# A two-layer float32 model on one Trainium2 core: the second layer's projections by seven block products, and one pass over chunks for queries, gates, u and retention

## The chip, the cores and the metric

The program runs on one core of one Trainium2 chip. The metric is device time of one execution in microseconds (us). Besides its runs, each kernel has one profiled execution, whose trace is read here. Engines: PE is TensorE, DVE VectorE, ACT ScalarE, POOL GpSimd; SP only issues DMAs.

## What is computed

Two layers over 2048 tokens of width 1024, all in float32. The first (pooling, two attentions, a gated feed-forward of width 2816) is touched only at its end. The second is this, cut down; its input is the output of the first layer, normalized once more:

```python
h = rmsnorm_2(x, g_pre) * (1.0 + scale[:, None, :]) + shift[:, None, :]
proj = jnp.einsum('bsd,de->bse', h, w_in)            # 1024 -> 7 x 512
gu, gv, gg, rq, rk, rv, rg = jnp.split(proj, PROJ_SPLITS, axis=-1)
# gmlp_branch, per chunk of 128 tokens and 4 groups of 128 channels
v = group_layernorm(v, ln_g); ws = w_s * causal[None]
mixed = jnp.einsum('gts,bnsgd->bntgd', ws, v) + b_s.T[None, None, :, :, None]
y_gmlp = u * mixed * jax.nn.silu(gate)
# retention_branch, 4 heads of 128
q = rotary(q, positions); k = rotary(k, positions) * (Dh ** -0.5)
scores = jnp.einsum('bnqhd,bnkhd->bhnqk', q, k) * decay_mask
intra = jnp.einsum('bnhqk,bnkhe->bnqhe', scores, v)
kv_chunk = jnp.einsum('bnkhd,bnkhe,kh->bnhde', k, v, k_decay)
def step(state, kv): return state * chunk_decay + kv, state
cross = jnp.einsum('bnqhd,bnhde,qh->bnqhe', q, states, q_decay)
y_ret = group_layernorm(intra + cross, gn_g) * jax.nn.silu(gate)
y = jnp.concatenate([y_gmlp, y_ret], axis=-1)
y = rmsnorm_2(jnp.einsum('bsm,md->bsd', y, w_out), g_post)
return x + gate[:, None, :] * y
```

## The kernel before

Every large product is made of three: both operands are split into a high and a low part (`split`, L123: ACT copies the high part, DVE subtracts it for the low one), and high x high, high x low and low x high are added up in PSUM. A product of 128 tokens, 1024 inputs and 512 columns is thus 24 matmuls of 128x512 (`mm3`, L148, lines L153 to L155, through `dense_N`).

The feed-forward (`phase2`) makes its products with `seven` (L995): a two by two block product by seven block products instead of eight. Its left side are seven stationary parts `l` (`stationary`, L970: three differences and one sum, seven splits, for each step of 256 tokens), its right side seven moving parts `r` (`moving`, L928: differences of the weight or activation blocks, L936, and fourteen splits of two k-blocks of 512), which stay for a whole group. The line of its matmuls is L1005; a step with 1024 inputs and two results of 512 columns for two token tiles is 84 matmuls. The partial sums are added by DVE (L1023, L1025, and in the `use` functions), and in `down` also by POOL (L1181). Each `r` part has one buffer, so at a change of the moving parts (a swap) the new part can be written only after the last product with the old one. `hidden` runs two halves of the tokens, `down` three groups of input channels (`FGROUPS`) by eight steps. Side work is put after products through the list `self.later`.

The second layer (`phase3`) goes by four blocks of 512 tokens (`second`, after `second_in` and `second_T`, which normalize, transpose (L194) and split). In each block the seven projections follow one another (`project`: gate, v, u, k, v, q, retention gate); their weights are loaded and split for every block (`wgroup`, tiles `ws`). Between them stand the mix (L1401) and, per chunk, the retention: heads transposed (L1430), scores (L1451), masked by DVE (L1454), cross product with the state (L1460), intra product (L1462), state update (L1470, L1474), group norm (L1323, L1324, POOL's root L175, L1486). The result is transposed (L1395) and the output projection is plain too (L1514 squares, L1515 gain, L1526 final sum). In this layer PE's work is 3456 matmuls of 128x512.

Who comes first on an engine is settled when the program is built, by a scheduler with priorities; each engine then runs its list in order.

## Time and profile before

| | before |
|---|---|
| three runs, median (lowest, highest) | 3651.73 us (3647.63, 3655.74) |
| profiled execution | 3649.51 us |
| its span in the trace | 3647.7 us |
| mean granted PE clock | 0.975 |
| PE busy | 94% |
| DVE, ACT, POOL busy | 67%, 43%, 25% |
| DMA traffic, mean | 516.77 MB, 142 GB/s |

Shares of busy time are means over stages. A matmul is recorded longer than the distance to the next one, since they overlap; to count what PE could do, the distance between starts is taken. The granted clock is given as a part of full speed; 0.5 is the lower of two levels, 1.2 GHz for 2.4.

### The profile page before, as it was taken

The numbers are of one execution on the slowest core, as the hardware profiler recorded it, in microseconds if no ns is written. First come the engines' busy times: TensorE is split into PE (matmuls) and PEld (weight loads), VectorE is DVE, ScalarE is ACT, GpSimd is POOL, SyncE is SP. The second block draws the span as 40 slices with busy tenths as digits, with TensorE's granted clock in tenths as the row PEclk, the third lists the DMA queues.
The fourth block names the chain that finished last, engine by engine and source line by source line (L and its number), as shares of the span: only waits on it lengthen the run. The fifth ranks groups of instructions, "written<-read, shape, count | busy, mean of one in ns | idle before, by whom it ended". The sixth has DMA issues, their size and how long they took to land. (4 is left out here: it accounts for less than half of the span.)

```text
span 3647.7 us, 46845 instructions
## 1 busy us (share of the span) xinstructions
PE 3435.5 (94%) x16704; PEld 2837.7 (78%) x16704; DVE 2455.8 (67%) x4104; ACT 1551.5 (43%) x2874; POOL 911.8 (25%) x1153
## 2 busy tenths in 40 slices
PE   6989989998889989999999998999969999999998
PEld 5777868887667877888778887878758878888887
DVE  8566674768888837666796668686856554655444
ACT  5346574657667634333433334232333332333322
POOL 4322243325652111110200002343521120221101
PEclk9999999999989999999999999999989999999999
DMA  5367655555433444333272334555563252332421
GB/s 168 122 208 225 184 158 179 191 156 179 149 107 113 136 145 143 104 101 110 94 233 75 104 118 136 171 177 172 182 230 115 70 180 87 129 125 75 159 90 64
DMA packets 397915, 516.77 MB, mean 142 GB/s; under 512 B 32449, under 2 KB 250225, under 8 KB 397681
## 3 DMA queue, kind: packets, MB, share of 16 engines
q1 hardware_dynamic: 357152, 384.73, 34.5%
q0 software_dynamic: 40528, 129.04, 9.9%
q8 instruction: 132, 2.16, 0.2%
q14 instruction: 103, 0.84, 0.1%
HBM read 385.98 MB, written 127.69 MB: 141 GB/s over the span
## 5 line engine op out<-in xcount | busy, mean ns | idle before, releaser
L1005 PE MATMUL acc<-r,l 128*128 128x512 f32 x6384 | 1477.9, 393 | 49.3 <-ACT l L126 8.8
L1005 PEld LDWEIGHTS acc<-r,l 128*128 128x128 f32 x6384 | 1203.9, 189 | 313.7 <-ACT l L126 14.8
L153 PE MATMUL d<-ws,h 128*128 128x512 f32 (+1 forms) x1280 | 508.5, 400 | 4.5 <-ACT b L1383 3.5
L154 PE MATMUL d<-ws,h 128*128 128x512 f32 (+1 forms) x1280 | 498.5, 391 | 0.0
L155 PE MATMUL d<-ws,h 128*128 128x512 f32 (+1 forms) x1280 | 496.4, 390 | 0.0
L127 DVE TENSOR_TENSOR ws<-raw,ws 128x1024 fp32r<-128x1024 f32 x216 | 272.9, 1266 | 217.4 <-ACT ws L126 214.2
L126 ACT ACTIVATE l<-sf 128x512 fp32r<-128x512 f32 (+1 forms) x312 | 192.9, 621 | 494.8 <-PE acc L1005 320.3
L126 ACT ACTIVATE ws<-raw 128x1024 fp32r<-128x1024 f32 x216 | 229.1, 1061 | 300.7 <-PE d L155 160.0
L126 ACT ACTIVATE l<-raw 128x512 fp32r<-128x512 f32 (+1 forms) x234 | 144.0, 618 | 361.2 <-PE acc L1005 353.3
L666 PE MATMUL s<-k,q 128*128 128x512 f32 (+2 forms) x960 | 272.7, 394 | 21.6 <-DVE s L697 6.2
L127 DVE TENSOR_TENSOR l<-sf,l 128x512 fp32r<-128x512 f32 (+1 forms) x312 | 234.3, 754 | 75.6 <-ACT l L126 73.6
L153 PEld LDWEIGHTS d<-ws,h 128*128 128x128 f32 x1280 | 243.2, 190 | 50.6 <-ACT b L1383 4.3
L155 PEld LDWEIGHTS d<-ws,h 128*128 128x128 f32 x1280 | 242.6, 190 | 48.6
L154 PEld LDWEIGHTS d<-ws,h 128*128 128x128 f32 x1280 | 243.2, 190 | 44.8 <-issue 1.0
L127 DVE TENSOR_TENSOR l<-raw,l 128x512 fp32r<-128x512 f32 (+1 forms) x234 | 174.8, 752 | 95.4 <-ACT l L126 95.2
L666 PEld LDWEIGHTS s<-k,q 128*128 128x128 f32 x960 | 167.2, 198 | 59.5 <-DVE s L697 14.1
L793 DVE TENSOR_TENSOR_SCAN s<-s,one 128x512 f32<-128x512 f32 (+3 forms) x160 | 188.2, 1208 | 21.6 <-ACT s L789 15.2
L1107 POOL DMA_DIRECT2D act<-wk x88 | 48.4, 550 | 583.8 <-DVE wk L1106 576.4
L704 ACT ACTIVATE s<-s,mx 128x128 f32<-128x128 f32 (+15 forms) x128 | 154.4, 1207 | 81.4 <-DVE mx L700 80.4
L725 PE MATMUL o<-v,pT 128*128 128x128 f32 x1088 | 149.3, 278 | 8.4 <-ACT pT L733 6.1
L725 PEld LDWEIGHTS o<-v,pT 128*128 128x128 f32 x1088 | 140.7, 193 | 19.4 <-ACT pT L733 10.3
L801 POOL TENSOR_TENSOR s<-s,s 128x1024 f32<-128x1024 f32 x48 | 123.5, 2573 | 72.7 <-DVE s L793 45.8
(277 smaller groups left out, 5330.8 us busy)
## 6 DMA issues: line engine op xcount, KB each, us to landing
raw<-in_w_in_dram SPq DMA_DIRECT2D x172, 512.0 KB, 4.2
raw<-in_w_out_dram SPq DMA_DIRECT2D x64, 512.0 KB, 4.3
k<-qkd SPq DMA_DIRECT2D x120, 256.0 KB, 4.2
q<-qkd SPq DMA_DIRECT2D x96, 256.0 KB, 4.4
wk<-x SPq DMA_DIRECT2D x96, 256.0 KB, 5.1
x<-wk POOLq DMA_DIRECT2D x96, 256.0 KB, 3.1
raw<-in_w_gate_dram SPq DMA_DIRECT2D x44, 512.0 KB, 3.8
...
```

Of the source, the lines that this page charges most:

```text
L126: nc.scalar.activation(hi, src, AF.Copy)
L127: nc.vector.tensor_tensor(out=lo, in0=src, in1=hi.bitcast(F32), op=ALU.subtract)
L153: self.nc.tensor.matmul(ps, st(0), mv(0), start=i == 0, stop=False)
L154: self.nc.tensor.matmul(ps, st(0), mv(1), start=False, stop=False)
L155: self.nc.tensor.matmul(ps, st(1), mv(0), start=False, stop=i == n - 1)
L666: nc.tensor.matmul(ps[:, :w], q[:, hl, c * P:(c + 1) * P], kt[:, o:o + w], start=hl == 0, stop=hl == 1 and not extra)
L704: nc.scalar.activation(e[:, :nk], e[:, :nk], AF.Exp, scale=-1.0, bias=mx[:, m, np_ - 1:np_], accum_out=s1[:, c, m:m + 1])
L725: nc.tensor.matmul(ops[:, c * P:(c + 1) * P], pT[:, j * P:(j + 1) * P], vs[kt // NT][:, kt % NT], start=kt == 0, stop=kt == nt - 1)
L793: nc.vector.tensor_tensor_scan(out=omb[:, c, :w][:, ::-1], data0=omb[:, c, :w][:, ::-1], data1=self.one.to_broadcast([P, w]), initial=1.0 ...
L801: nc.gpsimd.tensor_tensor(out=beta[:, two], in0=beta[:, two], in1=omb[:, two, 1:w + 1], op=ALU.mult)
L1005: nc.tensor.matmul(ps, l[lk][:, a, k], r[rk][:, b, k], start=first and k == 0 and i == 0, stop=k == nk - 1 and i == 2, skip_group_check=no ...
L1107: nc.gpsimd.dma_start(out=dst[:, j * TB:(j + 1) * TB], in_=s)
```

## The change

The second layer is cut anew. (1) Normalizing, transposing and writing its input (`h3_d`) is done by `second_rows`, as side work in the last group of `down` and in the first two steps after it. (2) `keys_values` makes the key and value projections with `seven` in eight steps of 256 tokens, rotates the keys and stores both. (3) `spatial` makes the gate and v projections of the gMLP with `seven`, and the mix, and stores the product with the gate. (4) The new `phase3` holds the split weights of q, retention gate and u in SBUF and makes one pass over sixteen chunks of 128 tokens: three plain products of 24 matmuls, and the retention of the chunk. (5) `phase4` makes the output projection with `seven`, with the final norm and sum. Besides, `moving` takes its blocks in another order and makes all differences on DVE, a piece of side work may spread over several products, and `FGROUPS` is turned round, so that the last group of `down` has eight blocks of 128 inputs.

```diff
-FGROUPS = (8, 8, 6)
+FGROUPS = (6, 8, 8)
...
             self.phase2()
-            self.pri.update(w=1000, x=1000)
             self.phase3()
+            self.phase4()
...
+        a = get(0, 0)
+        r["11"] = part("11", a)
+        b = get(0, 1)
+        less(a, b, a)
+        r["t1"] = part("t1", a)
+        for p in range(len(pieces)):
+            (c, n), u = pieces[p], get(1, 1, p)[0]
+            for o in (a[p], b[p]):
+                nc.vector.tensor_tensor(out=o[:, :n], in0=u[:, :n], in1=o[:, :n], op=ALU.subtract)
+        r["t2"] = part("t2", a)
+        r["t3"] = part("t3", b)
         r21 = get(1, 0)
-        if not first:
-            r["21"] = part("21", r21)
-            r["22"] = part("22", r22)
-        t4 = t2
-        less(t4, r21, t2, nc.gpsimd)
-        r["t4"] = part("t4", t4)
+        r["21"] = part("21", r21)
+        less(a, r21, a)
+        r["22"] = part("22", get(1, 1))
+        r["t4"] = part("t4", a)
...
-            for f in todo:
-                f()
+            self.later = [g for g in todo if next(g, None)] + self.later
...
+            self.load_rows()
             for g in range(len(FGROUPS)):
                 self.down(g)
+            self.keys_values()
+            self.spatial()
...
+            else:
+                self.l = self.second_stationary(self.h3_d, 0)
...
-        if not last_g:
-            with self.tc.high_priority(500):
-                self.r = self.down_moving(g + 1)
+            if last_g and s < n - 2:
+                self.later.append(self.second_rows(s))
+        with self.tc.high_priority(500):
+            self.r = self.down_moving(g + 1) if not last_g else self.second_moving("w_in_2", 4 * TB, 5 * TB)
...
+    def token_steps(self, src, use, follow, rows=False):
+        nc = self.nc
+        for s in range(S // (2 * P)):
+            l, r = self.l, self.r
+            if s < S // (2 * P) - 1:
+                self.l = self.second_stationary(src, s + 1)
+            elif follow is not None:
+                self.l = follow[0]()
+            if rows and s < 2:
+                self.later.append(self.second_rows(6 + s))
+            def total(i, j, keep=False):
+                def f(z, ps):
+                    o = self.t(self.wk, [P, TB], "wk") if keep else z
+                    nc.vector.tensor_tensor(out=o, in0=ps, in1=z, op=ALU.add)
+                    use(2 * s + i, j, o)
+                return f
+            self.seven(l, r, KC // 2, lambda ps: use(2 * s, 0, ps), total(0, 1), total(1, 0), total(1, 1, True))
+        self.flush()
+        if follow is not None:
+            with self.tc.high_priority(500):
+                self.r = follow[1]()
+    def keys_values(self):
+        nc = self.nc
+        wk = lambda: self.t(self.wk, [P, TB], "wk")
+        def use(t, j, o):
+            psum = t % 2 == 0 and j == 0
+            if j == 0:
+                d = wk()
+                self.rotate(d, t, o, wk(), not psum)
+                o = d
+            nc.gpsimd.dma_start(out=(self.kr_d, self.vr_d)[j][t], in_=o)
+        self.token_steps(self.h3_d, use, (lambda: self.second_stationary(self.h3_d, 0), lambda: self.second_moving("w_in_2", 2 * TB, TB)), True)
+    def spatial(self):
...
+            if j == 1:
+                mv = self.group_stats([o[:, g * P:(g + 1) * P] for g in range(4)], "gs")
+                r = self.rsqrt_mean(mv[:, :, 1], 4, 1.0)
...
+                nc.gpsimd.tensor_tensor(out=off, in0=mv[:, :, 0], in1=r[:, :4], op=ALU.mult)
...
+                for g in range(4):
+                    c = o[:, g * P:(g + 1) * P]
+                    nc.scalar.activation(c, c, AF.Identity, scale=r[:, g:g + 1], bias=off[:, g:g + 1])
+                nc.gpsimd.tensor_tensor(out=o, in0=o, in1=lng, op=ALU.mult)
+            else:
...
+                nc.scalar.activation(s, o, AF.Silu)
...
+            have[t, j] = o
+            if (t, 1 - j) in have:
+                v, g_ = have.pop((t, 1)), have.pop((t, 0))
+                def mix():
+                    ps = self.t(self.tp2, [P, TB], "tp2")
+                    for g in range(4):
+                        c = slice(g * P, (g + 1) * P)
+                        nc.tensor.matmul(ps[:, c], wsT[:, c], v[:, c], start=True, stop=True)
+                    for g in range(4):
+                        c = slice(g * P, (g + 1) * P)
+                        nc.vector.scalar_tensor_tensor(out=g_[:, c], in0=ps[:, c], scalar=bs[:, g:g + 1], in1=g_[:, c],
+                                                       op0=ALU.add, op1=ALU.mult)
+                    nc.gpsimd.dma_start(out=self.m_d[t], in_=g_)
+                self.later.append(once(mix, 4))
+        self.token_steps(self.h3_d, use, None)
...
+    def phase3(self):
...
+            def queries(t):
+                x = self.token_tile(self.h3_d, t, self.rawh, "rawh")
+                h = self.t(self.hl3, [P, 2, KC, P], "hl", F32R, align=512)
+                self.split(h[:, 0], h[:, 1], x)
+                kr, vv, m, q = (tmp() for _ in range(4))
+                for o, src in ((kr, self.kr_d), (vv, self.vr_d), (m, self.m_d)):
+                    nc.sync.dma_start(out=o, in_=src[t])
+                self.rotate(q, t, product("q", h), tmp(), False)
+                return h, kr, vv, m, q
+            new, last = queries(0), None
+            for t in range(n):
+                h, kr, vv, m, q = new
+                gate = tmp()
+                def gates():
+                    nc.scalar.activation(gate, product("g", h), AF.Silu)
+                    nc.gpsimd.tensor_tensor(out=gate, in0=gate, in1=self.gng, op=ALU.mult)
+                def units():
+                    nc.vector.tensor_tensor(out=m, in0=product("u", h), in1=m, op=ALU.mult)
+                if t < n - 1:
+                    gates()
+                steps = self.retention(q, kr, vv, t == n - 1)
+                next(steps)
+                if last is not None:
+                    self.chunk_out(*last)
+                if t < n - 1:
+                    units()
+                next(steps)
+                if t < n - 1:
+                    new = queries(t + 1)
+                else:
+                    units()
+                    gates()
+                self.turned(t, 0, m)
+                y = drain(steps)
+                last = t, y, gate
+            self.chunk_out(*last)
...
+        kT, qT = heads_T(kr), heads_T(q)
+        for h, c in enumerate(H if not end else ()):
+            nc.gpsimd.tensor_scalar(out=kr[:, c], in0=kr[:, c], scalar1=self.kdec[:, h:h + 1], scalar2=None, op0=ALU.mult)
+        sp = self.t(self.pm, [P, TB], "m")
+        for c in H:
+            nc.tensor.matmul(sp[:, c], kT[:, c], qT[:, c], start=True, stop=True)
+        sT = tmp()
+        nc.vector.tensor_tensor(out=sT, in0=sp, in1=self.ret_mask.rearrange("p h q -> p (h q)"), op=ALU.mult)
+        yield
+        op = self.t(self.pm, [P, TB], "m")
+        old = self.state
+        if old is not None:
+            for h, c in enumerate(H):
+                nc.tensor.matmul(op[:, c], qT[:, c], old[:, c], start=h == 0, stop=False)
+        new = None
+        if not end:
             kp = self.t(self.pm, [P, TB], "m")
+            new = self.t(self.tmp, [P, TB], "state", bufs=2)
+        for h, c in enumerate(H if not end else ()):
+            nc.tensor.matmul(kp[:, c], kr[:, c], vv[:, c], start=True, stop=True)
+            if old is None:
+                nc.vector.tensor_copy(new[:, c], kp[:, c])
+            else:
+                nc.vector.scalar_tensor_tensor(out=new[:, c], in0=old[:, c], scalar=CHUNK_DECAY[h], in1=kp[:, c], op0=ALU.mult,
+                                               op1=ALU.add)
+        self.state = new
+        for h, c in enumerate(H):
+            nc.tensor.matmul(op[:, c], sT[:, c], vv[:, c], start=old is None and h == 0, stop=h == RH - 1)
+        yield
+        y = tmp()
+        nc.scalar.activation(y, op, AF.Copy)
+        mv = self.group_stats([y[:, c] for c in H], "rn")
+        vq = self.t(self.tiny, [P, 4], "vq")
+        nc.gpsimd.tensor_tensor(out=vq, in0=mv[:, :, 1], in1=self.qdec2, op=ALU.mult)
...
+    def phase4(self):
+        nc, a = self.nc, self.a
+        with ExitStack() as es:
+            self.block_pools(es, last=True)
+            with self.tc.high_priority(700):
+                self.l = self.second_stationary(self.yT_d, 0)
+            with self.tc.high_priority(500):
+                self.r = self.second_moving("w_out_2", 0, TB)
+            gout = self.t(self.c3, [P, D], "wide")
...
                 junk = self.t(self.tiny, [P, TB], "junk3", mybir.dt.bfloat16, bufs=1)
+                nc.scalar.activation(junk, src, AF.Square, scale=D ** -0.5, accum_out=ss[:, j:j + 1])
+                nc.vector.tensor_tensor(out=y[:, c], in0=src, in1=gout[:, c], op=ALU.mult)
...
+                nc.gpsimd.tensor_scalar(out=m, in0=ss[:, 0:1], scalar1=ss[:, 1:2], scalar2=EPS, op0=ALU.add, op1=ALU.add)
+                nc.gpsimd.tensor_tensor(out=r, in0=m, in1=self.mhalf[:, :1], op=ALU.pow)
+                for h in range(2):
+                    c = slice(h * TB, (h + 1) * TB)
+                    nc.vector.scalar_tensor_tensor(out=y[:, c], in0=y[:, c], scalar=r, in1=res[:, c], op0=ALU.mult, op1=ALU.add)
+                    (nc.sync if t >= S // P - 2 else nc.gpsimd).dma_start(out=self.out[0, t * P:(t + 1) * P, c], in_=y[:, c])
...
+            self.token_steps(self.yT_d, use, None)
```

Line numbers of the new program are its own: `split` is L133 and L134, `less` and the differences L949 and L980, `stationary`'s sums L1001, `seven` L1025, L1042 and L1044, the plain products L160 to L162.

**PE where the second layer starts.** `acc` are PSUM tiles, `pp` those of the transposes, `d` those of the plain products. Before, after the last products of `down`:

```order
L1005 MATMUL acc_23646<-r_22747,l_23542 128x512 x9
L1005 MATMUL acc_23710<-r_22752,l_23547 128x512 x9
L1005 MATMUL acc_23682<-r_22759,l_23550 128x512 x9
L194 MATMUL pp_23871<-c_ident,x_23825 128x128
L194 MATMUL pp_23871<-c_ident,x_23827 128x128
L194 MATMUL pp_23871<-c_ident,x_23829 128x128
L194 MATMUL pp_23871<-c_ident,x_23831 128x128
L153 MATMUL d_23973<-ws_23955,h_23876 128x512
```

Now, where `down` gives way to keys and values (the `r` tiles are the new moving parts, `l_241` are stationary parts of the first step, `l_243` of the second):

```order
L1025 MATMUL acc_24516<-r_24358,l_24135 128x512
L1025 MATMUL acc_24632<-r_24309,l_24372 128x512 x12
L1025 MATMUL acc_24401<-r_24347,l_24130 128x512 x5
L1025 MATMUL acc_24653<-r_24320,l_24377 128x512 x12
L1025 MATMUL acc_24516<-r_24358,l_24135 128x512 x11
L1025 MATMUL acc_24666<-r_24333,l_24382 128x512 x12
L1025 MATMUL acc_24471<-r_24363,l_24138 128x512 x12
L1025 MATMUL acc_24702<-r_24338,l_24387 128x512 x12
L1025 MATMUL acc_24747<-r_24358,l_24395 128x512 x12
```

Transposes of the layer's input, which stood between `down` and the first projection, are gone from the seam, and products of the second step stand between those of the first.

**DVE inside the retention.** `d` is a plain product, `m` a small one, `ws` and `hl` are splits. Before, around one chunk:

```order
L1474 SCALAR_TENSOR_TENSOR state_28395<-state_26896,m_28394 128x128
L1421 TENSOR_TENSOR tmp_28452<-tmp_28452,tmp_28453 128x4x64
L1422 TENSOR_TENSOR tmp_28452<-tmp_28452,tmp_28453 128x4x64
L127 TENSOR_TENSOR ws_28707<-raw_28705,ws_28707 128x1024
L1464 TENSOR_SCALAR b_28011<-b_28011,c_ret_kdec 128x128 x4
L127 TENSOR_TENSOR ws_28939<-raw_28937,ws_28939 128x1024
L1323 BN_STATS rn_s_28405<-b_28013 128x6 x4
L1474 SCALAR_TENSOR_TENSOR state_28395<-state_26896,m_28394 128x128
L1454 TENSOR_TENSOR tmp_28477<-m_28472,c_ret_mask 128x512
L1419 TENSOR_TENSOR tmp_28550<-d_28525,c_cos 128x512
L1420 TENSOR_TENSOR tmp_28551<-d_28525,c_sin 128x512
L1324 BN_AGGR rn_m_28406<-rn_s_28405 128x2 x4
```

Now, one chunk of the pass:

```order
L1597 SCALAR_TENSOR_TENSOR state_29297<-state_29113,m_29296 128x128
L1405 TENSOR_TENSOR tmp_29318<-d_29322,rot_6184_29348 128x512
L1406 TENSOR_TENSOR tmp_29347<-d_29322,rot_6185_29350 128x512
L1407 TENSOR_TENSOR tmp_29318<-tmp_29318,tmp_29347 128x4x64
L1408 TENSOR_TENSOR tmp_29318<-tmp_29318,tmp_29347 128x4x64
L1472 BN_STATS rn_s_29366<-tmp_29364 128x6 x4
L1597 SCALAR_TENSOR_TENSOR state_29297<-state_29113,m_29296 128x128
L1473 BN_AGGR rn_m_29367<-rn_s_29366 128x2 x4
L1611 TENSOR_SCALAR tmp_29364<-tmp_29364,rn_m_29367,vq_29376 128x128 x4
L1558 TENSOR_TENSOR tmp_29364<-tmp_29364,tmp_29203 128x512
L1597 SCALAR_TENSOR_TENSOR state_29297<-state_29113,m_29296 128x128
L1581 TENSOR_TENSOR tmp_29438<-m_29433,c_ret_mask 128x512
```

The splits of weights are gone; rotation, statistics, norm (L1611), product with the gate (L1558), last state update (L1597), mask (L1581) and the product with u (L1526) of one chunk stand in one row.

**DVE ahead of the output projection.** `r` and `stg` are moving parts and their blocks, `raw_63` the first stationary blocks. Before, from the last retention norm to the first output tile:

```order
L1474 SCALAR_TENSOR_TENSOR state_30374<-state_30307,m_30373 128x128
L1496 TENSOR_TENSOR b_29729<-b_29729,rg_30535 128x512
L127 TENSOR_TENSOR ws_30590<-raw_30588,ws_30590 128x1024
L1474 SCALAR_TENSOR_TENSOR state_30374<-state_30307,m_30373 128x128
L127 TENSOR_TENSOR ws_30707<-raw_30705,ws_30707 128x1024
L127 TENSOR_TENSOR y_30543<-tp_30538,y_30543 128x512
L127 TENSOR_TENSOR y_30551<-tp_30546,y_30551 128x512
L127 TENSOR_TENSOR y_30559<-tp_30554,y_30559 128x512
L127 TENSOR_TENSOR y_30567<-tp_30562,y_30567 128x512
L1515 TENSOR_TENSOR b_30570<-d_30593,c_gout 128x512
```

Now, from the last chunk's statistics to the first split of a stationary part:

```order
L1472 BN_STATS rn_s_30410<-tmp_30408 128x6 x4
L134 TENSOR_TENSOR r_30593<-stg_30535,r_30593 128x1024
L1473 BN_AGGR rn_m_30411<-rn_s_30410 128x2
L949 TENSOR_TENSOR stg_30537<-stg_30575,stg_30537 128x1024
L1473 BN_AGGR rn_m_30411<-rn_s_30410 128x2 x3
L134 TENSOR_TENSOR r_30577<-stg_30575,r_30577 128x1024
L134 TENSOR_TENSOR r_30588<-stg_30584,r_30588 128x1024
L134 TENSOR_TENSOR r_30593<-stg_30537,r_30593 128x1024
L1611 TENSOR_SCALAR tmp_30408<-tmp_30408,rn_m_30411,vq_30420 128x128 x4
L134 TENSOR_TENSOR r_30588<-stg_30586,r_30588 128x1024
L1558 TENSOR_TENSOR tmp_30408<-tmp_30408,tmp_30307 128x512
L1001 TENSOR_TENSOR sf_30509<-raw_6377_30504 128x512
```

Where four splits of finished outputs and a few of weights stood, there are now five splits and a difference of moving parts, the end of the last chunk, and the stationary parts of the first step.

## Rows read from the trace of the kernel before

**Rows 1.** Page, the span and busy time by engine (us, share of the span, instructions).
```profile
span 3647.7 us, 46845 instructions
...
PE 3435.5 (94%) x16704; PEld 2837.7 (78%) x16704; DVE 2455.8 (67%) x4104; ACT 1551.5 (43%) x2874; POOL 911.8 (25%) x1153
```

**Rows 2.** Stretches: from:to, us, busy us of each engine (instructions), PEclk, DMA share, GB/s.
```profile
2584.00:2680.00 96.00, 96.00 (x424) 79.06 (x423) 72.06 (x114) 26.23 (x51) 42.52 (x49) 1.00 0.61 199
2680.00:2734.00 54.00, 24.32 (x98) 17.41 (x97) 28.85 (x33) 20.51 (x33) 10.75 (x15) 0.68 0.70 254
2734.00:2964.00 230.00, 226.14 (x1088) 186.63 (x1088) 131.23 (x256) 79.28 (x116) 37.24 (x52) 1.00 0.37 119
```

**Rows 3.** Groups of PE, 2686 to 3648: count, busy us, mean ns, idle before.
```profile
L153 PE MATMUL d<-ws,h 128*128 128x512 f32 x896 | 354.8, 399 | 3.8 <-ACT b L1383 3.5 <-ACT h L126 0.3
...
L153 PE MATMUL d<-ws,y 128*128 128x512 f32 x256 | 101.2, 395 | 4.5 <-DVE b L1515 3.8 <-ACT y L126 0.3
...
L1460 PE MATMUL m<-state,tmp 128*128 128x128 f32 x120 | 22.0, 279 | 1.1 <-DVE state L1474 1.1
...
L1401 PE MATMUL m<-b,c_wsT 128*128 128x512 f32 x32 | 15.0, 592 | 0.0
```

**Rows 4.** Timeline of PE: start us, us, engine, line, operation, count [idle before <-releaser].
```profile
2685.11 1.78 PE L1005 MATMUL acc<-r,l 128*128 128x512 f32 x4
2707.83 0.48 PE L194 MATMUL pp<-c_ident,x 128*128 128x128 f32 x1 [20.94 <-DVE x L1341]
...
2805.15 1.03 PE L1395 MATMUL tp<-c_ident,b 128*128 128x128 f32 x8
...
3108.27 1.06 PE L1462 MATMUL m<-b,tmp 128*128 128x128 f32 x8
...
3640.74 0.39 PE L155 MATMUL d<-ws,y 128*128 128x512 f32 x1
```

**Rows 5.** Stretches around the four changes of the moving parts, columns as in group 2.
```profile
1790.00:1850.00 60.00, 52.98 (x229) 42.12 (x228) 60.00 (x68) 26.64 (x39) 18.98 (x7) 1.00 0.51 168
2240.00:2285.00 45.00, 35.55 (x145) 27.57 (x144) 40.85 (x47) 15.23 (x23) 20.91 (x15) 0.96 0.68 218
2395.00:2435.00 40.00, 34.14 (x133) 26.67 (x132) 38.88 (x39) 17.80 (x24) 19.74 (x12) 0.91 0.53 171
2555.00:2600.00 45.00, 41.01 (x175) 31.98 (x174) 43.04 (x57) 17.82 (x31) 23.75 (x20) 1.00 0.45 147
```

**Rows 6.** Groups of DVE and POOL: three in `down` (2430 to 2555), three in a block (2734 to 2964).
```profile
L127 DVE TENSOR_TENSOR l<-sf,l 128x512 fp32r<-128x512 f32 x27 | 22.8, 849 | 10.6 <-ACT l L126 10.5
L127 DVE TENSOR_TENSOR l<-raw,l 128x512 fp32r<-128x512 f32 x20 | 18.3, 937 | 0.1
...
L1181 POOL TENSOR_TENSOR wk<-wk,wk 128x512 f32<-128x512 f32 x21 | 29.7, 1424 | 38.5 <-DMA wk<-x 20.0 <-DVE wk L1025 18.3
...
L175 POOL TENSOR_TENSOR rs_r<-rs_m,mhalf 128x4 f32<-128x4 f32 x10 | 10.7, 1070 | 0.8
...
L1323 DVE BATCH_NORM_STATS2 gs_s<-b 128x6 f32<-128x128 f32 x16 | 3.5, 278 | 0.7 <-ACT b L1372 0.6
...
L1324 DVE BATCH_NORM_AGGREGATE gs_m<-gs_s 128x2 f32<-128x6 f32 x16 | 1.6, 155 | 0.0
```

**Rows 7.** Timelines: PE at the swap inside `down`, POOL and DVE at the swap inside `hidden`.
```profile
2407.66 9.42 PE L1005 MATMUL acc<-r,l 128*128 128x512 f32 x33 [2.92 <-DVE wk L1175]
...
1809.70 6.77 POOL L936 TENSOR_TENSOR stg<-stg,stg 128x1024 f32<-128x1024 f32 x1 [10.44 <-DVE r L127]
...
1808.41 3.48 DVE L127 TENSOR_TENSOR r<-stg,r 128x1024 fp32r<-128x1024 f32 x3
1811.81 0.68 DVE L127 TENSOR_TENSOR l<-sf,l 128x512 fp32r<-128x512 f32 x1
1812.41 0.68 DVE L127 TENSOR_TENSOR l<-raw,l 128x512 fp32r<-128x512 f32 x1
...
1814.75 2.80 DVE L127 TENSOR_TENSOR r<-stg,r 128x1024 fp32r<-128x1024 f32 x1
```

423 lines of the change are left out of this document (185 added, 238 removed).

## The prediction

> **What bounds the kernel now.** The page comes first: TensorE (PE) is busy 94% of a span of 3647.7 us [rows 1], so the time is first a count of matmuls and then what PE loses between them. The table by stretches shows where [rows 2]: in the last group of `down`, and in a whole block of the second layer, PE is full (96.00 of 96, 226.14 of 230), while VectorE (DVE) has 72.06 of 96 and 131.23 of 230. Only the seam between the two, 2680 to 2734, has PE at 24.32 of 54 and a granted clock of 0.68. So DVE, ScalarE (ACT) and DMA are off the path inside the stages and on it at seams.
>
> **The price of a matmul.** In the full stretch of `down` 424 starts of 128x512 stand in 96 us [rows 2], 0.2264 each; I take 0.227, which allows for a record that is missing. Eight records of the small F32 kind take 1.06 us of which the last one's 0.28 laps over, so 0.112 a record, two records to a product; eight transposes take 1.03 with 0.27, so 0.109 each [rows 4].
>
> **The second layer now.** The last products of `down` end at 2685.11 + 1.78 = 2686.9 [rows 4], the last of them having started some 0.6 before; from that start, 2686.3, to the end of the span at 3647.7 are 961 us. Its content: (896 + 256) x 3 = 3456 matmuls [rows 3] x 0.227 = 784.5; the four retention products of L1451, L1460, L1462, L1470, together 504 records, x 0.112 = 56.4; 384 transposes 41.9; the mix L1401, 32 wide records, about 12. Sum 895. The other 66 are losses: the seam about 33 (PE starts its next work 20.94 us after the last product [rows 4], works in pieces and at the lower level, 1.2 GHz, for part of the time until about 2730: 54 us hold only 98 records [rows 2]); the tail 6.6 (last matmul at 3640.74); some 27 over four blocks.
>
> **What the change takes away.** The key, value, gate, v and output products go through `seven`: 84 matmuls for 96. Four projections of 384 and the output projection's two halves of 384 are 2304, and become 2016; q, the retention gate and u keep 1152. So 288 matmuls fewer, 288 x 0.227 = **-65.4**. Retention loses eight records (-0.9), the mix goes from 32 wide to 128 narrow ones, 14.3 for 12 (+2). Transposes stay 384. Content: -64. The old seam goes, **-33**: norms and transposes of the second layer run inside the last `down` group, whose PE is full, and its next stage starts with products that need only `l` and `r` tiles (first order lists). The four blocks' own 27 go too, and are replaced below. Weights of the plain products are split once and not four times, 12 wide splits where there were 144; DVE was off the path there, so this counts for nothing by itself.
>
> **What it adds: seams.** *Swaps.* Two further changes of the moving parts, `down` to keys and values, and those to the spatial stage. There are four of the kind in the trace [rows 5]. Counting starts against one per 0.227 us, they lose 60/0.227 - 229 = 35 starts or 8.0 us, then 53 or 12.1, 43 or 9.8 and 23 or 5.3. In all four DVE is at 91 to 100%: fourteen splits of 1.16 us (three in 3.48 [rows 7]) and eight differences of the same width, some 26 us, on top of the stage's work. The new stages leave DVE less room (below), so I take the dearest, 12 each: **+24**, bounds 5 and 20 (20 is those 26 us with only a quarter of DVE free). That `moving` gives its differences to DVE alone, where half were POOL's, I cost at nothing: one of POOL's lasted 6.77 us beside DVE's splits [rows 7], so what DVE gains in work it saves in waiting.
>
> *Spatial stage to chunk pass.* The program's PE order has the last two mixes ahead of the first q product. The last v goes through a sum, statistics, POOL's root (1.07 us), four scalings on ACT, a multiplication on POOL (1.42) [rows 6]: about 7 us with nothing waiting, and ACT has splits of the new weights queued ahead. I take 9.4 idle and 4 at the lower level: **+13.5**, bounds 4 (one chain, half hidden) and 33 (the old seam).
>
> *Chunk pass to output projection.* In the DVE order (third pair of lists) five splits and one difference of the new moving parts stand between the last chunk's statistics and its end, and the first `l` split behind all of them: 6 x 1.16 + 4 x 0.28 + 4 x 0.16 + four norms of some 0.3, and three of 0.68: 12 us. With the wait for POOL's root and its small companions (2) and for the intra product and its copy ahead of it (2.5) I take 16.5, and 3.5 at the lower level: **+20**, bounds 8 and 33.
>
> *Tail.* One sum more ahead of the same chain: +1.
>
> **What it adds: in the stages.** DVE's load per step of 256 tokens, 84 x 0.227 = 19.1 us of PE: seven splits, four sums for the stationary parts, five sums of products, all of 512 columns, 0.68 [rows 7]: 10.9. POOL's products lengthen what runs beside them: in `down` 20 splits mean 0.937 and 27 mean 0.849 where 0.68 is the rule, 9.7 us beside 21 POOL products [rows 6, 7], 0.46 for each. Keys and values add the rotation (three operations of 512 columns, four of 256 taken as half): 3.5 and 0.5, 14.9 of 19.1 or 79%. The spatial stage adds 8 statistics pairs (0.28 + 0.16 [rows 6]), 8 mix operations of 128 columns, taken as 0.28 too, and two POOL products beside it: 17.6 of the 20.9 that PE has there with the mixes, 85%. The output projection adds four products with the gain and four final ones: 16.4 of 19.1, 86%. The nearest rows with PE full have DVE at 75% [rows 2], the nearest with PE starved at 91 and more [rows 5]; mine lie between, so some loss: 2 in the last `down` group, 3, 4 and 4, against 0 and 45 (every stage bound by DVE at a tenth over). The chunk pass has DVE at about 10.4 of 21.7 us per chunk, less than in the old blocks, so it loses as they did: 9. Together **+22**.
>
> A rule speaks against this. POOL's products stand beside a DVE that is nearly full. In the trace a POOL difference ran 6.77 us while DVE's splits went on, and then a split of DVE took 2.80 instead of 1.16 [rows 7]: each waited for the other. The sum holds 0.46 us per POOL product for it. The Trainium skill, page "SBUF — State Buffer", section "SBUF: two separate sides", calls the shared ports an exclusive lock held for the whole instruction; the trace agrees, and by that rule each of the spatial stage's 16 products would cost DVE the whole 1.42 us [rows 6], 16 x 0.96 = 15 us more if DVE were the bound there, and the sum would be 3623.
>
> **The sum.** -64 - 33 - 27 + 24 + 13.5 + 20 + 1 + 22 = -43.5. The profiled execution took 3649.5 us, so 3606; the median of the runs is 2.2 above it, so **3608**. About 0.2%, 7.3 us, is what a measurement of this kernel can tell from no change.
>
> **The rivals.**
> *Cheap seams.* Swaps at 5.3 each (-13), seams of 4 and 8 (-22) and half of the stage losses (-11): 3562 in all, some 3580 if half of that comes true. For it: the second swap inside `down` cost 5.3 [rows 5], and the program interleaves products of two steps around a swap. Against: DVE is fuller in the new stages. Chance 0.15.
> *DVE binds the stages.* Swaps at 20 (+16), seams at 28 (+22), DVE a few per cent over in three stages (+12): 3658 if all come true, 3640 with most. For it: DVE at 91 to 100% [rows 5]. Against: DVE back to back starts faster than its durations say (two of 0.68 us start 0.60 apart [rows 7]). Chance 0.17.
> *Slower: one stall per chunk.* On DVE the norm of a chunk (L1611, which waits for POOL's root), its product with the gate, the fourth state update and the masking L1581 stand in one row (second order lists), and PE's cross and intra products wait for the last two. From the end of a q product DVE needs 2.1 for the rotation, 1.8 for statistics, about 2 while POOL works, four norms and a product, some 8.5 us with the update, and PE reaches its scores after 24 + 21 matmuls and 12 transposes, 11.5 us, and the intra products 3 later. So cover is 3 to 6 us; if the chain is longer by more, every chunk stalls. A stall in the trace idled PE 2.92 us, and the 33 matmuls behind it took 9.42, (9.42 - 0.39)/32 = 0.282 each, 1.8 us more than at full clock [rows 7]: 4.7 together, x 16 = 75: **3683**. It decides from (43.5 + 7.3)/16 = 3.2 us lost per chunk. For it: POOL has four more operations per chunk than before (the decays), and its small ones take longer beside DVE. Against: the cover. Chance 0.10.
> *It does not do what it says* is excluded for the count: the program lists 8400 matmuls of `seven` where there were 6384, and 1152 plain ones where there were 3456 in this layer.
>
> **How the numbers follow.** Forecast 0.58, cheap 0.15, DVE-bound 0.17, stall 0.10. Range 3580 to 3640: it leaves out the stall and part of both middle cases, about 2 in 10. Faster by over 0.2% (below 3644.4): forecast, cheap, and 0.10 of DVE-bound, 0.83. Within 0.2%: 0.07. Slower: 0.10.
>
> **What would show it.** Right: no seam of 20 us after `down`, two swaps of about 12 us with DVE at 95% or more, chunks of 21.7 to 22.3 us, seams of 10 to 20 us before and after the chunk pass at a granted clock below 1. Wrong: chunks of 25 us with PE waiting for L1581 or the state; spatial or output steps longer than 21.5 and 19.6 with DVE full; or seams beyond 30.

## The result, and the profile after

The changed kernel takes 3613.15 us (median of four runs, 3607.01 to 3613.39) against 3650.03 before (3647.63 to 3655.74): a ratio of 0.9893, with a 95% interval from 0.9876 to 0.991. Forecast were 3608 in a range of 3580 to 3640. The time and the direction came out; two terms of the sum did not, and with the stages, which lost less than was forecast, they nearly cancel.

First the page of the changed kernel, for [rows 1]:

```profile
span 3611.6 us, 47629 instructions
...
PE 3373.2 (93%) x16504; PEld 2789.0 (77%) x16504; DVE 2532.7 (70%) x4289; ACT 1628.9 (45%) x3136; POOL 1007.0 (28%) x1397
```

PE is busy 62 us less, with 200 records fewer, and the span is 36.1 us shorter: about 26 us of what was taken from PE came back as waiting. Where, the stretches tell (columns as in [rows 2]; the stages are, in this order, the last `down` group from its second step on, the swap to keys and values, the second step of keys and values, its rest, the swap to the spatial stage, the spatial stage, its seam to the chunk pass, the pass, its seam to the output projection, and that):

```profile
2560.00:2700.00 140.00, 124.38 (x546) 99.72 (x545) 91.03 (x117) 87.44 (x177) 70.47 (x108) 0.94 0.71 242
2700.00:2740.00 40.00, 29.77 (x122) 21.49 (x121) 36.64 (x41) 24.27 (x40) 14.56 (x12) 0.91 0.78 251
2740.00:2790.00 50.00, 40.10 (x176) 32.06 (x175) 37.48 (x54) 30.87 (x63) 22.05 (x34) 0.86 0.70 230
2790.00:2860.00 70.00, 70.00 (x311) 57.95 (x310) 55.89 (x89) 19.69 (x34) 17.29 (x23) 1.00 0.44 142
2885.00:2925.00 40.00, 33.37 (x136) 26.18 (x135) 38.81 (x55) 18.44 (x25) 13.58 (x5) 0.91 0.53 159
2960.00:3060.00 100.00, 100.00 (x483) 84.20 (x482) 69.95 (x186) 40.18 (x81) 36.69 (x56) 1.00 0.23 77
3060.00:3110.00 50.00, 36.99 (x179) 31.00 (x178) 29.78 (x57) 21.15 (x29) 14.59 (x18) 0.86 0.57 180
3110.00:3410.00 300.00, 300.00 (x1643) 256.02 (x1642) 119.71 (x327) 61.14 (x96) 97.47 (x152) 1.00 0.30 92
3410.00:3450.00 40.00, 24.14 (x131) 20.30 (x130) 31.67 (x56) 18.08 (x23) 10.78 (x14) 0.83 0.53 164
3450.00:3600.00 150.00, 150.00 (x656) 123.99 (x655) 114.85 (x180) 57.97 (x123) 42.00 (x56) 0.99 0.45 148
```

Inside the new stages PE is full, at a granted clock of 0.99 to 1.00, with DVE at 80% (55.89 of 70), 70% and 77%. The swaps and seams lose what was forecast. But the first and the third line are no seams, and there PE idles: the last `down` group and the second step after it, both of which carry the side work `second_rows`. DVE is busy 65% and ACT 62% of the first line, so neither is full.

The seam before the output projection is the one that was read from the order of DVE. In the timeline of the changed kernel (first PE, then DVE):

```profile
3429.99 1.06 PE L1601 MATMUL m<-tmp,tmp 128*128 128x128 f32 x8
3445.46 1.09 PE L1551 MATMUL tp<-c_ident,tmp 128*128 128x128 f32 x4 [14.41 <-DVE tmp L1558]
...
3434.01 0.86 DVE L1472 BATCH_NORM_STATS2 rn_s<-tmp 128x6 f32<-128x128 f32 x4
3434.79 1.50 DVE L134 TENSOR_TENSOR r<-stg,r 128x1024 fp32r<-128x1024 f32 x1
3436.21 0.17 DVE L1473 BATCH_NORM_AGGREGATE rn_m<-rn_s 128x2 f32<-128x6 f32 x1
3437.10 1.23 DVE L949 TENSOR_TENSOR stg<-stg,stg 128x1024 f32<-128x1024 f32 x1 [0.72 <-DMA stg<-in_w_out_dram]
...
3440.19 2.36 DVE L134 TENSOR_TENSOR r<-stg,r 128x1024 fp32r<-128x1024 f32 x2 [0.53 <-ACT r L133]
3442.47 1.11 DVE L1611 TENSOR_SCALAR tmp<-tmp,rn_m,vq 128x128 f32<-128x128 f32 x4
3443.49 1.22 DVE L134 TENSOR_TENSOR r<-stg,r 128x1024 fp32r<-128x1024 f32 x1
3444.63 0.68 DVE L1558 TENSOR_TENSOR tmp<-tmp,tmp 128x512 f32<-128x512 f32 x1
```

PE's last intra products start at 3429.99 and its next work at 3445.46. In between the chunk's statistics, norm and product stand among the splits of the new moving parts: 11.3 us from the first statistics to the end of L1558, where 12 were counted.

How the losses are counted, here and below: the time between the first starts of two steps, less 0.227 us for each 128x512 matmul, 0.109 for each transpose and 0.112 for each small record that starts in it, the prices of the prediction.

| us | forecast | changed kernel |
|---|---|---|
| content of PE | -64 | -64 |
| losses of the old second layer (seam, blocks, tail) | -66.6 | -66.6 |
| swap to keys and values, swap to the spatial stage | 24 | 13.0 + 9.5 |
| seam to the chunk pass | 13.5 | 15.5 |
| seam to the output projection | 20 | 18.2 |
| tail | 7.6 | 8.8 |
| in the spatial stage, chunk pass, output projection | 4 + 9 + 4 | 0.1 + 3.2 + 1.4 |
| in the last `down` group and in keys and values | 2 + 3 | 27.6 + 14.1 |
| ahead of the last `down` group | 0 | -17 |
| sum | -43.5 | -36 |

The last but one line is 13.1 us by the first product of `down` (of these some 4.5 by the end of the attention, where little of the code is touched) and 4 after it: some 1 by the swaps into its three groups, and 3 that the kernel before lost ahead of the last products of `down`, just before the point from which the prediction counts the old seam.

### The profile page after: what moved, and what is told of

Same layout as the page of the kernel before. It is cut to its first block, busy times and chain, and to the rows that moved or that the text cites. A ratio compares the mean times of both kernels' runs of the same rounds, so it can differ in the third digit from the quotient of the medians.

```text
span 3611.6 us, 47629 instructions
## 1 busy us (share of the span) xinstructions
PE 3373.2 (93%) x16504; PEld 2789.0 (77%) x16504; DVE 2532.7 (70%) x4289; ACT 1628.9 (45%) x3136; POOL 1007.0 (28%) x1397
## 4 chain that ended last, share of the span: by engine, by line
PE 64%; DVE 12%; DMA 4%; issue 4%; ACT 2%; POOL 2%; SPq 0%; DVEq 0%; POOLq 0%; ACTq 0%
PE acc L1025 39%; PE d L160 5%; PE d L162 5%; PE d L161 5%; PE o L738 3%; PE s L679 3%; DVE s L806 2%; DVE r L134 2%; DVE l L134 1%; PE tp L744 1%; DMA wk<-x 1%; DVE stg L980 1%; DVE pT L134 1%; POOL s L814 1%; PE tp L833 1%
## 5 line engine op out<-in xcount | busy, mean ns | idle before, releaser
L1025 PE MATMUL acc<-r,l 128*128 128x512 f32 x8400 | 1961.8, 394 | 68.3 <-ACT r L133 26.0
L1025 PEld LDWEIGHTS acc<-r,l 128*128 128x128 f32 x8400 | 1587.8, 190 | 420.9 <-ACT r L133 36.4
L133 ACT ACTIVATE l<-sf 128x512 fp32r<-128x512 f32 (+1 forms) x408 | 252.8, 623 | 585.7 <-PE acc L1025 414.2
L133 ACT ACTIVATE l<-raw 128x512 fp32r<-128x512 f32 (+1 forms) x306 | 190.1, 623 | 443.3 <-PE acc L1025 425.0
L134 DVE TENSOR_TENSOR l<-sf,l 128x512 fp32r<-128x512 f32 (+1 forms) x408 | 295.6, 727 | 79.7 <-ACT l L133 77.6
L134 DVE TENSOR_TENSOR l<-raw,l 128x512 fp32r<-128x512 f32 (+1 forms) x306 | 219.7, 721 | 119.1 <-ACT l L133 118.9
L133 ACT ACTIVATE r<-stg 128x1024 fp32r<-128x1024 f32 (+1 forms) x120 | 121.1, 1030 | 122.4 <-DMA stg<-in_w_in_dram 23.0
L160 PE MATMUL d<-ws,h 128*128 128x512 f32 (+1 forms) x384 | 153.2, 401 | 0.7 <-DVE h L213 0.7
L1001 DVE TENSOR_TENSOR sf<-raw 128x512 f32<-128x512 f32 (+1 forms) x102 | 73.1, 717 | 112.7 <-DMA raw<-in_w_up_dram 47.2
L134 DVE TENSOR_TENSOR r<-stg,r 128x1024 fp32r<-128x1024 f32 (+1 forms) x120 | 145.4, 1224 | 3.1 <-ACT r L133 3.1
L162 PE MATMUL d<-ws,h 128*128 128x512 f32 (+1 forms) x384 | 146.8, 384 | 0.0
L161 PE MATMUL d<-ws,h 128*128 128x512 f32 (+1 forms) x384 | 146.3, 383 | 0.0
L1205 POOL TENSOR_TENSOR wk<-wk,wk 128x512 f32<-128x512 f32 x72 | 113.0, 1580 | 117.4 <-DMA wk<-x 85.1
L826 PE MATMUL o<-pT,v 128*128 128x512 f32 (+3 forms) x320 | 119.4, 411 | 14.8 <-DVE pT L134 9.8
```

The lines of the kernel that those rows point to most:

```text
L133: nc.scalar.activation(hi, src, AF.Copy)
L134: nc.vector.tensor_tensor(out=lo, in0=src, in1=hi.bitcast(F32), op=ALU.subtract)
L160: self.nc.tensor.matmul(ps, st(0), mv(0), start=i == 0, stop=False)
L161: self.nc.tensor.matmul(ps, st(0), mv(1), start=False, stop=False)
L162: self.nc.tensor.matmul(ps, st(1), mv(0), start=False, stop=i == n - 1)
L826: nc.tensor.matmul(ops[:, c0 * P:], vs[kb][:, j], aT[hl][:, :n], start=diag and j == 0 and hl == 0, stop=kb == 0 and j == NT - 1 and hl == 1)
```

## The experiments

All runs were timed beside the kernel before on their own chip. Its median there was 3650.64 for the first four, 3648.27 for the next four, 3650.78 for three more and 3650.02 for the last. The first four ask whose the 42 us and the 17 us are.

**e1_no_rows: the side work away.** `second_rows` does nothing; the stages of the second layer read `hT_d`, and the residual reads `x2_d`.

```diff
     def second_rows(self, s):
+        return
+        yield
...
-                self.l = self.second_stationary(self.h3_d, 0)
+                self.l = self.second_stationary(self.hT_d, 0)
...
```

> The changed kernel without its side work second_rows: norms, transposes and the stores of h3 and xf are left out (the second layer's stages read the feed-forward's input hT, the residual reads x2, both already in DRAM and of the same shape). In the changed kernel the stretch from 2560 to 2707.5 loses 27.8 us against its matmuls, and 2735 to 2790 loses 14.3. Theory (the side work makes both losses: PE's list stands behind its transposes and behind late results): 128 transposes less are 14 us, and some 35 to 42 us of losses go, 3613 becomes 3557 to 3566; the last down group's stretches show PE full. Rival (the losses belong to the stage itself, to eight input blocks per step, to the swap and to a DVE near 85%): only the 14 us of transposes go, 3595 to 3600.

3558.2 us, 55 less. The last `down` group is full again in its table by stretches, with DVE at 72%:

```profile
2530.00:2660.00 130.00, 129.50 (x564) 107.09 (x565) 93.49 (x125) 37.33 (x59) 45.19 (x49) 0.99 0.59 189
```

Step by step nothing is left in it but the swaps: 12.0 into the last group, 11.1 and 9.1 at the two new ones, and 0.5 at most in any other step. So the 42 us are the side work's, and with its 128 transposes it costs 55.

**e2_own_out: the transposed rows in buffers of their own.**

```diff
-        for x, (b, r) in zip(xn, at):
+        for x, y, (b, r) in zip(xn, xs, at):
...
-                o = self.t(self.wk, [P, NT, P], "wk")
+                o = y[:, h * TB:(h + 1) * TB].rearrange("p (k t) -> p k t", k=NT)
```

> One part of the side work alone: the transposed rows go into the buffers that held the norms (xs) and not into four of the nine wk buffers. Theory of the buffers (SP's loads wk<-x for the down products wait for a wk buffer that the stores h<-wk still hold, so that L1199 comes late, 4.2 us at 2658 to 2662 with some 2 us at the lower clock behind it): the waits of acc for L1199 (6.0 us in the stretch) go and 6 to 12 us with them, 3601 to 3607. Rival (the DMA is late for another reason, or ACT's list is what is late): 3611 to 3615, and the waits stand elsewhere.

3614.22 us. The waits that the changed kernel shows (PE, 2555 to 2800: what it waited for, us in total, times, longest)

```profile
PE tp L1347 <- ACT wk L1350: 9.9, 7, 4.0
PE acc L1025 <- DVE r L134: 6.8, 3, 5.3
PE acc L1025 <- ACT wk L1031: 6.7, 2, 4.7
PE acc L1025 <- DVE wk L1199: 6.0, 2, 4.2
```

have become others in this run: L1199 is gone from them as the theory wanted, and another came for it.

```profile
PE tp L1347 <- DVE stg L1339: 18.0, 5, 11.8
PE acc L1025 <- ACT r L133: 7.5, 6, 2.5
```

**e3_spread: four transposes after a product, not eight.**

```diff
-            yield True
+                yield True
```

> One part of the side work alone: the generator yields after each half of a token tile, so that four transposes and not eight come after one product. Theory of the PSUM banks (two tp2 banks, ACT empties a bank in four pieces of 0.37 us, so the third group of four transposes waits 1.3 us and more with PE's list behind it): the waits of tp for L1350 (9.9 us in the two stretches) go and 6 to 14 us with them, 3599 to 3607. Rival (ACT is late with everything, at some 84% of the step, and a later transpose waits as long): 3611 to 3617.

3611.3 us: 2 less, within the noise. The waits of `tp` for L1350 fell from 9.9 to 3.0 us, and those for ACT's splits of `r` rose from 2.7 to 10.4.

**e4_old_new_moving: the new `moving` in the kernel before.** `moving` and `loaded` are taken over whole, and nothing else.

```diff
...
-        t3 = r12
-        less(t3, r22, r12, nc.gpsimd)
...
+        for p in range(len(pieces)):
+            (c, n), u = pieces[p], get(1, 1, p)[0]
+            for o in (a[p], b[p]):
+                nc.vector.tensor_tensor(out=o[:, :n], in0=u[:, :n], in1=o[:, :n], op=ALU.subtract)
...
-        less(t4, r21, t2, nc.gpsimd)
+        less(a, r21, a)
...
```

> The kernel before with one part of the change: the new moving (order of the blocks, all differences on DVE). In the traces the changed kernel gains 3.2 us at the start of hidden, 5.3 at the swap inside hidden and some 6 in the swaps of down before the second layer begins. Theory (the new moving makes these gains: POOL's differences of 3.6 to 6.8 us stood in a swap's chain): 3650 becomes 3636 to 3642, and the swap's stretch inside hidden loses 3 us instead of 8. Rival (they come from the other pools, the turned FGROUPS or from chance): 3648 to 3652.

3622.23 us: 28 less, twice what the theory gave it, and three quarters of what the whole change gave. The four swaps of [rows 5] are now these, in the same table, shifted by what was gained before:

```profile
1780.00:1840.00 60.00, 56.68 (x249) 46.22 (x248) 60.00 (x77) 27.97 (x41) 2.16 (x4) 1.00 0.59 193
2220.00:2265.00 45.00, 42.59 (x186) 34.41 (x185) 41.76 (x54) 19.01 (x27) 11.63 (x14) 1.00 0.75 245
2380.00:2420.00 40.00, 36.16 (x149) 28.96 (x150) 40.00 (x46) 15.76 (x21) 14.18 (x14) 0.96 0.81 263
2530.00:2575.00 45.00, 44.47 (x194) 35.85 (x193) 42.48 (x63) 18.09 (x33) 23.29 (x21) 1.00 0.58 190
```

Counted as before they lose 15, 12, 27 and 4 starts, 13 us in all, where they lost 35, 53, 43 and 23, 35 us. DVE is as full as it was; POOL falls from 18.98 to 2.16 us in the first of them. So 22 of the 28 us lie in these four stretches. Another 7.0 are gained by the last score product of the attention (1269.69 for 1276.67), ahead of which only the first moving parts are made; no run tells the cause of this part.

The next four ask which part of either does it.

**e5_late_rows: the side work begins nine products after its step, not four.**

```diff
-        for _ in range(4 if s < 6 else 0):
+        for _ in range(9 if s < 6 else 0):
```

> The changed kernel with each piece of side work begun nine products after its step and not four, so that its loads stg<-x stand later in SP's list. In the changed kernel, 2555 to 2707, SP waited 22.0 us in those loads for the stores x<-wk of the same rows (longest 9.2), and the loads of down's partial sums and of stationary blocks stand behind them. Theory (SP's list in order is what spoils the last down group: a load that waits for a store holds all loads behind it): the waits of L1319 go, and 15 to 30 us with them, 3583 to 3598. Rival (ACT and DVE near 85% with any side work make the losses; three changes of place have the same sum of losses): 3609 to 3617, losses of 36 to 45 us again at other places.

3596.33 us, the least of all runs that compute everything: a ratio of 0.9866 to the kernel before (0.985 to 0.9882), whose interval still meets that of the changed kernel. The time lies in the theory's range, but its reason does not hold: in the profiled execution (at 3606.61 the slowest of the four) SP still waited 16.5 us in L1319 for the stores, and the losses were 16.2 in the group, 17.4 and 10.3 after it.

**e6_old_dve: the kernel before, its two POOL differences on DVE.**

```diff
-        less(t3, r22, r12, nc.gpsimd)
+        less(t3, r22, r12)
...
-        less(t4, r21, t2, nc.gpsimd)
+        less(t4, r21, t2)
```

> The kernel before with the two POOL differences of moving put on DVE and nothing else. The whole new moving gave 28 us there. Theory (the engine: POOL's 128x1024 differences, 3.6 to 6.8 us each beside DVE, stand in the chain to t3 and t4 at each of five swaps): most of it, 18 to 28 us, 3622 to 3633. Rival (the order of the blocks: the last part to be ready is another one, and each difference is made as soon as its piece has landed): under 8 us, 3643 to 3651.

3626.38 us: 22 of the 28 us are the engine's. The 6 that are left for the order are less than these two runs, each with its own interval, can tell apart. The four swaps now lose 25, 18, 31 and 4 starts, 18 us:

```profile
1780.00:1840.00 60.00, 56.27 (x239) 45.38 (x238) 60.00 (x76) 29.16 (x41) 2.71 (x5) 0.97 0.51 162
2220.00:2265.00 45.00, 42.75 (x180) 34.27 (x179) 41.63 (x52) 21.03 (x29) 6.81 (x7) 0.96 0.58 181
2380.00:2420.00 40.00, 36.17 (x145) 28.59 (x145) 40.00 (x45) 19.13 (x25) 16.45 (x9) 0.91 0.57 176
2530.00:2575.00 45.00, 44.20 (x194) 35.98 (x193) 42.84 (x65) 21.75 (x37) 21.49 (x15) 1.00 0.53 170
```

**e7_rows_in_sbuf: the rows of six steps never leave SBUF.** DVE's last sums go into the tiles of the side work; no store of them and no load. The squares go to scratch tiles, and xf is scaled and stored in halves.

```diff
...
+                o = place(i, j, t)
-                    nc.vector.tensor_tensor(out=t, in0=ps, in1=t, op=ALU.add)
-                    store(i, j, t)
+                    nc.vector.tensor_tensor(out=o, in0=ps, in1=t, op=ALU.add)
+                    if not stay:
+                        store(i, j, t)
...
```

> The changed kernel with the rows of the last down group kept in SBUF: DVE's last sums go straight into the tiles that the side work reads, so for six of eight steps neither the store x<-wk nor the load stg<-x is there (12 MB less traffic, 12 loads less on SP's list, 24 stores less on POOL's). ACT, DVE and PE do the same work. Theory (SP's list): the losses of the last group fall from 28 to under 12, 3585 to 3600. Rival (ACT's and DVE's load): 3608 to 3616.

3605.52 us, between the ranges of theory and rival. The group itself loses 31.5 us, now waiting for sums that DVE makes late; the two steps after it lose 8.6 and 7.5 instead of 13.0 and 14.1.

```profile
PE acc L1025 <- DVE wk L1042: 14.0, 6, 5.1
PE acc L1025 <- ACT r L133: 6.7, 4, 4.4
PE acc L1025 <- DVE stg L1220: 6.4, 6, 2.9
```

**e8_one_evac: less work for ACT.** Left out are the gain and shift of the second layer's input.

```diff
-                for k in range(NT):
-                    kc = h * NT + k
-                    nc.scalar.activation(o[:, k], ps[:, k * P:(k + 1) * P], AF.Identity, scale=self.gpre[:, kc:kc + 1],
-                                         bias=self.shift[:, kc:kc + 1])
+                nc.scalar.activation(o.rearrange("p k t -> p (k t)"), ps, AF.Copy)
```

> The changed kernel without the gain and shift in the side work: each bank of four transposes is emptied by one ACT copy of 512 columns (0.6 us) in place of four scaled pieces (1.48), which takes 64 x 0.9 = 57 us off ACT in some 200 us. Theory (ACT's load of 84% in the last group is what makes the losses): half of the 42 us go, 3588 to 3597. Rival (SP's list is): 3606 to 3615, since the loads wait as before.

3610.47 us, within the noise of the changed kernel: a lighter ACT alone does not mend it. ACT was less full than the expectations said, 62% in the last group by the table above and not 84%, and this run took 26 us from it, not 57 (152.4 to 126.3 us busy from 2540 to 2790, nearly all of the side work's time).

The last four divide the side work itself.

**e9_light_rows: no norm chain.** Loads, transposes, one copy for each bank and the stores of `h3` stay; the products, squares, scalings, roots and the stores of `xf` are left out.

```diff
-        for i in range(2):
-            nc.vector.tensor_tensor(out=xn[i], in0=xs[i], in1=self.gf, op=ALU.mult)
...
-            nc.scalar.activation(xs[i], xn[i], AF.Copy, scale=r1[:, i:i + 1])
-            nc.gpsimd.dma_start(out=self.xf_d[b][r:r + P], in_=xs[i])
...
```

> The changed kernel with the norm chain left out of the side work: per row tile no product with the gain, no two squares, no scaling, no store of xf and no POOL roots; what stays are the loads stg<-x, the transposes, one ACT copy for each bank, and the stores of h3 (the residual reads x2). Theory (the work that the side work puts into ACT's, DVE's and POOL's lists is what holds back the results that PE waits for, wherever one wait is mended): 30 of the 42 us of losses go, 3578 to 3588. Rival (loads that wait for stores on SP's list, and transposes in PE's list): at most 12 us go, 3600 to 3611.

3576.05 us, 37 less. Two of the four `stg` tiles that a piece of side work holds, of five in all, are no longer taken either. The group loses 0.2 us and the second step after it 4.8; the swaps stay. And this with SP's list waiting longer than in the changed kernel. Its waits, 2555 to 2707, first in the changed kernel,

```profile
SPq L1319 <- DMA x<-wk: 22.0, 6, 9.2
```

then in this run:

```profile
SPq L1319 <- DMA x<-wk: 34.4, 10, 6.7
```

So loads that wait for stores, and the transposes, cost by themselves no more than some 5 us of the 42.

**e10_late_spread: e5 and e3 together.**

```diff
-        for _ in range(4 if s < 6 else 0):
+        for _ in range(9 if s < 6 else 0):
...
-            yield True
+                yield True
```

> Two parts of the side work together: begun nine products after its step (which gave 17 us alone) and a yield after each bank of four transposes (which gave 2 alone). Theory (pieces that are thinner and later meet fewer results that PE waits for): 3588 to 3596. Rival (each cure only moves a wait): 3596 to 3604.

3604.08 us, 8 more than e5 alone; the ratios to the kernel before, 0.9881 and 0.9866, have intervals that overlap. The group loses 11.0, the two steps after it 21.4 and 8.6.

**e11_late_pool: e5 with the loads on POOL's queue.**

```diff
...
-            nc.sync.dma_start(out=x, in_=self.x2_d[b][r:r + P])
+            nc.gpsimd.dma_start(out=x, in_=self.x2_d[b][r:r + P])
```

> The late start with the loads stg<-x on POOL's queue in place of SP's; nine products after its step the row's stores have long landed, so POOL should not wait. Theory of SP's list (the loads of partial sums, stationary and moving blocks stand behind stg<-x): another 6 to 15 us go, 3581 to 3591. Rival (SP's list is not what holds PE back): 3594 to 3602.

3611.33 us: more than either range. SP has no such wait any more, the group loses 12.9, and the step of the swap 26.8. With e9 this ends the theory that these loads in SP's list hold PE back.

**e12_no_chain: the norm's instructions without its chain.** The gain product reads the gain twice, both squares read the row's tile, the scalings take a constant: the second layer's input is not the normalized row.

```diff
-            nc.vector.tensor_tensor(out=xn[i], in0=xs[i], in1=self.gf, op=ALU.mult)
+            nc.vector.tensor_tensor(out=xn[i], in0=self.gf, in1=self.gf, op=ALU.mult)
...
-            nc.scalar.activation(xs[i], xn[i], AF.Copy, scale=r1[:, i:i + 1])
+            nc.scalar.activation(xs[i], xn[i], AF.Copy, scale=self.gpre[:, i:i + 1])
...
```

> The changed kernel with all instructions of the side work but without the norm's chain between them: DVE's gain product reads the gain alone, both squares read the loaded row, and ACT's and DVE's scalings take a constant in place of POOL's roots (so the second layer's input is not the normalized row). Loads, stores, transposes and every width stay. Without the norm chain (runs above) the losses were gone although SP waited as long. Theory (it is the waits of the chain in the in-order lists of ACT and DVE, not its work): 20 to 35 of the 42 us go, 3578 to 3593. Rival (the work itself, some 57 us on ACT, 32 on DVE): 3604 to 3614.

3606.83 us, 6 less, which is no more than noise: the rival's range. But a wait of the list is still there, only another one. Of ACT, 2555 to 2707, in the changed kernel:

```profile
ACT stg L1326 <- DVE stg L1324: 14.8, 7, 7.3
```

and in this run, where the square no longer waits for the product but directly for the load:

```profile
ACT stg L1326 <- DMA stg<-x: 35.3, 8, 7.0
```

The losses side by side, from each run's profiled execution:

| us lost | last group, steps 2 to 8 | first step after | second and third step after | median time |
|---|---|---|---|---|
| changed kernel | 27.6 | 13.0 | 14.2 | 3613.15 |
| e1 no side work | 0.0 | 11.1 | 0.0 | 3558.2 |
| e2 own buffers | 31.6 | 21.3 | 0.1 | 3614.22 |
| e3 spread | 26.0 | 13.7 | 9.3 | 3611.3 |
| e5 late | 16.2 | 17.4 | 10.4 | 3596.33 |
| e7 rows in SBUF | 31.5 | 8.6 | 9.3 | 3605.52 |
| e8 one copy a bank | 20.2 | 21.6 | 7.1 | 3610.47 |
| e9 no norm chain | 0.2 | 11.7 | 4.8 | 3576.05 |
| e10 late and spread | 11.0 | 21.4 | 8.7 | 3604.08 |
| e11 late, POOL's queue | 12.9 | 26.8 | 12.2 | 3611.33 |
| e12 no chain | 20.2 | 18.4 | 5.5 | 3606.83 |

## Why the prediction was right, and where it was not

**The count of PE.** Right: 288 matmuls for 65 us, and chunks of 21.91 us where 21.7 to 22.3 were given.

**Swaps and seams.** Right in size, all five: 13.0, 9.5, 15.5, 18.2 and 8.8 against 12, 12, 13.5, 20 and 7.6. The last seam was right by its mechanism, DVE's order; its 12 us were 11.3. The swaps were right in part by luck. Their 12 us were taken from four swaps of the kernel before, and a full DVE was named as the cause; e4 and e6 show DVE just as full at the same swaps, which lose 13 and 18 us where they lost 35. So half of that price and more was POOL's differences, which the change takes away. Why the swaps of the changed kernel, without them, still lose 9.5 to 13.4 us is not shown.

**Stages with DVE at 80%.** The sum gave them 4, 9 and 4 and they lost 0.1, 3.2 and 1.4. DVE's load was counted too high in two of them, 85% and 86% where the table has 70% and 77%; in keys and values the 79% were 80%, and there PE stays full beside it over 70 us, where the rows before ended at 75% [rows 2]. With this the rival in which DVE binds the stages is out. So are the 15 us more in the spatial stage: they were to come if DVE was the bound there, and it was not.

**The side work.** The step that failed was "2 in the last `down` group, 3", by the load of DVE: it was 41.7 us (27.6 + 14.1). The prediction had said that the norms run "inside the last `down` group, whose PE is full", as if that were a cover. PE's fullness says nothing about ACT, DVE and POOL, whose lists the norm chain was put into, and a share of 62 or 65% says nothing about when a list is free. e1 shows that the 42 us are the side work's; e9 that 37 of them go with its norm part; e2, e3, e7, e8, e11 and e12 each take one wait or one load away and leave most of the sum standing elsewhere. What is shown is therefore that the norm part, on three engines that also make the operands of the next products, holds PE back. e9 also takes away the stores of `xf` and half of the staging tiles, and no run parts these from the chain. One place shows how it can happen, in the second step after the group (ACT, then DVE, then PE):

```profile
2759.51 1.06 ACT L1326 ACTIVATE stg<-stg 128x1024 f32<-128x1024 f32 x1 [4.39 <-DVE stg L1324]
2768.63 0.68 ACT L1031 ACTIVATE wk<-acc 128x512 f32<-128x512 f32 x1
...
2758.25 1.23 DVE L1324 TENSOR_TENSOR stg<-stg,wide 128x1024 f32<-128x1024 f32 x1 [2.10 <-DMA xf<-stg]
...
2762.11 1.11 PE L1347 MATMUL tp<-c_ident,stg 128*128 128x128 f32 x4 [4.04 <-ACT wk L1350]
2769.36 6.85 PE L1025 MATMUL acc<-r,l 128*128 128x512 f32 x19 [4.75 <-ACT wk L1031]
```

ACT stands 4.39 us at a square of the chain, ahead of which DVE's product, by the trace, waited for a store of `xf` to free its tile. Then come 9 us of ACT's work, most of it the side work's, and only behind this the copy L1031 that PE waits for. Here it is a wait and then work. All runs that keep the squares have ACT wait at them, 21.0 us in the changed kernel and 21.0 to 36.6 in the others (2535 to 2795), but the losses do not follow that sum: it is 35.0 in e5, which loses less than the changed kernel. So whether the chain costs more by its work or by its waits stays open; e12 took one wait out and let in another. It stays open too why e5 gained 17 us, since neither e10 nor e11, built on it, kept that.

**The new `moving`.** The other step that failed was "That `moving` gives its differences to DVE alone, where half were POOL's, I cost at nothing". Alone in the kernel before the new `moving` is worth 28 us (e4), 22 by the engine (e6). The row that should have told it stood in the prediction: one difference on POOL ran 6.77 us [rows 7], the longest of those at the swaps, where DVE's own take 1.22, and t3 and t4, which came from these, were needed at each swap. The argument that DVE saves in waiting what it gains in work agrees with e4, where DVE is no fuller, and left out that the part is ready sooner, by up to some 5 us (6.77 less 1.22, an estimate). The Trainium skill, page "SBUF — State Buffer", section "SBUF: two separate sides", describes an exclusive lock between DVE and GpSimd, which is POOL here. The trace agrees with it, 6.77 us and 2.80 us for two operations side by side [rows 7], and it speaks for this part of the change, where the prediction used it only against another.

In the changed kernel 17 us are gained outside the second layer, of which 4.5 lie in the attention; how much of the 17 is the work of `moving` is argued from e4 and not shown, since no run puts the old one back there. Its swaps into the second and third group of `down` lose 13.4 and 10.9, where the kernel before lost 8.5 and 5.3 and e4 loses 6.3 and 0.8. The changed kernel has five staging buffers where e4 has six, and its groups come in another order; neither was tried by itself.

**The sum.** The two failures are +37 and -17, the stages -12, and the rest within 3: -43.5 became -36. That the forecast came within 5 us of the median is luck: without the 17 it would have been some 22 us too low, and without the 37 some 32 too high. The rival with a stall in every chunk did not come: chunk after chunk takes 21.91 us.

No run was faster beyond doubt than the changed kernel among those that compute everything; e5's median is 17 us lower, with intervals that touch.
